# A hybrid encoder block on one core: the weights of five projections stored block by block

## The chip, the cores and the metric

The kernel runs on one core of a Trainium2 chip. The time is the device time of one execution in microseconds (us); smaller is better. The core has five engines, each with its own queue of instructions: TensorE (PE in the profile; PEld is its weight load), VectorE (DVE), ScalarE (ACT), GpSimd (POOL) and SyncE (SP), which only issues transfers. Transfers run on 16 DMA engines, whichever queue issued them. TensorE multiplies out of SBUF, the on-chip memory of 128 partitions, into PSUM.

## The reference

The input x is 2048 tokens of 1024 numbers, float32. One layer is computed:

```
h      = rms_norm(x, pre_mix_g)
proj   = h @ w_in                     # 1024 -> 5376: attention 1536, RWKV 1792, gates 2048
y_a    = chunk_band_attention(q, k, v, rel_bias)       # 8 heads, own chunk of 64 and 8 before it
y_b    = rwkv7_time_mix(p_rwkv, ...)                   # 8 heads, a delta-rule state over time
merged = sigmoid(gate_a) * (y_a @ proj_a) + sigmoid(gate_b) * (y_b @ proj_b)   # 512 -> 1024 each
x      = x + rms_norm(merged @ w_out, post_mix_g)      # 1024 -> 1024
u      = square(relu(rms_norm(x, pre_ffn_g) @ w_up)) @ w_down   # 1024 -> 4096 -> 1024
x      = x + rms_norm(u, post_ffn_g)
```

## The kernel before

**Precision.** Matrix products keep float32 accuracy by splitting each operand into a high and a low part. ScalarE casts the high part, VectorE subtracts to get the low one (`split`, L68), and `mm3` (L72) issues three products: high x high, high x low, low x high.

**Groups.** Tokens are worked on in four groups of 512 (`run`, L1480 on). For each group the RWKV branch comes first, then attention, then the merge with the branch projections and the output projection. The norm of the next group and the residual of the one before run in between. After the last group follows the feed-forward network, in two halves of two groups: `phase_up` (w_up) and a down phase (w_down) each. Both use sums and differences of quarter matrices to save products; the sums (`td`, t1 to t4 in the profile) and the activations (`ad`, `sd`) pass through DRAM.

**Where the weights come in.** Every weight block is 512 KB and is loaded by one transfer on SP's queue into a raw tile of 128 partitions x 1024 numbers (`wraw`); then it is split into `whi` and `wlo`, or in the up stage into `a1h`, `s12h` and so on. For w_in a block is 128 columns and all 1024 rows, eight rows to a partition (`block`, L82). For the branch projections it is 256 columns and 512 rows, for the output projection 256 rows and half of the columns (`blocks`, L85), for w_up 128 columns again (`load`, L1139). In DRAM the weights are the plain matrices, so a block's part of one partition lies in several pieces, one for each row.

**What sets the order.** The first group loads each block where it is used (`dense`, L109) and notes the order. From then on `ahead` (L99) runs one block in front: it loads and splits the next block before it hands over the present one. The pool has two raw tiles and two of each split tile, so a load waits for the split of the block two before it. In the feed-forward stages the raw tiles come from a pool of four, shared with the loads of w_down and of the activations.

The program is written in one order; a planner then fills each engine's queue when the program is built. It plays the program through with prices of its own for every instruction and transfer and takes what is ready first, so instructions of different steps can change places on an engine. Each engine runs its queue strictly in the order that came out. On ScalarE the casts of weights, the casts of `bl` (input of an up stage, L1090), the evictions of PSUM (`o` at L1002, `z` at L1190) and the activations stand in one line.

**Early in the program** the table of the attention bias is written out to DRAM by eight transfers (`build_bias`, L899) that share SP's queue with the first weight loads.

`layout` (L1536 on) arranges the inputs on the host before the launch: it drops the depth axis, reverses the bias table and flattens one vector. Its time is not part of the measurement.

Of the kernel before, what the change touches and what calls it, by code (L numbers as in the profile page):

```python
# [17 lines left out]
P = 128  # L18
D = 1024
KB = D // P  # L20
FF = 4096
HW = 512
NP = 4
# [29 lines left out]
class Block:  # L53
# [26 lines left out]
        return mm  # L80

    def block(self, col):  # L82
        return self.a["w_in"][:, col : col + P].rearrange("(k p) n -> p k n", p=P), KB, P

    def blocks(self):  # L85

        a = self.a
        for g in range(self.NG):
            if g:
                yield from map(self.block, self.order)  # L90
            for w in (a["proj_b"], a["proj_a"]):
                for i in range(KB // 2):
                    yield w[:, 2 * i * P : (2 * i + 2) * P].rearrange("(k p) n -> p k n", p=P), NP, 2 * P
            for n in range(2):
                for k in range(0, KB, 2):
                    rows = a["w_out"][k * P : (k + 2) * P, n * 512 : (n + 1) * 512]
                    yield rows.rearrange("(k p) n -> p k n", p=P), 2, 512

    def ahead(self):  # L99

# [1001 lines left out]
    def phase_up(self, half, zp, rp, cb, pn, early, sums=False):  # L1102
# [4 lines left out]
        tc, nc, a = self.tc, self.nc, self.a  # L1107
        KH = KB // 2
        lo4, hi4 = slice(0, KH), slice(KH, KB)
        with ExitStack() as ctx:  # L1110
# [27 lines left out]

            def load(fb):  # L1139
                raw = rp.tile([P, KB, P], F32, tag="raw", name="wraw")  # L1140
                nc.sync.dma_start(raw, a["w_up"][:, fb * P : (fb + 1) * P].rearrange("(k p) n -> p k n", p=P))
                return raw

            def parts(src, tag, n):
# [43 lines left out]
            for i in range(early):  # L1188
                A11, A12 = parts(load(2 * i), ("a1", "s12", "s3")[i % 3], KB)
                nc.scalar.copy(z[:, i], product(A11, B11, self.pd, "d"))  # L1190
                hidden(z[:, i], product(A12, B21, self.pd, "d"), 2 * i, 0)
                advance(ops, 1 + i % 2)
            advance(ops)

            for i in range(FF // P // 2):
                raw0, raw1 = load(2 * i), load(2 * i + 1)
                (a11, a12), (a21, a22) = ((x[:, lo4], x[:, hi4]) for x in (raw0, raw1))
                if i >= early:
# [24 lines left out]
                w = up.tile([P, G], F32, tag="w", name="w")  # L1223
# [312 lines left out]
def layout(inputs):  # L1536
    import numpy as np

    got = {}
    for name in _INS:  # L1540
        v = np.asarray(inputs["rel_bias" if name == "rel_rev" else name])[0]
        if name == "rel_rev":
            v = v[:, ::-1]
        if name == "r_k":
            v = v.reshape(-1)
        got[name] = np.ascontiguousarray(v)
    return got

# [16 lines left out]
```

## Time and profile before

| What | Value |
|---|---|
| time, median of 3 runs | 3363.93 us (3361.67 to 3368.97) |
| time of the profiled execution | 3364.64 us |
| its span, first to last instruction | 3362.8 us |
| TensorE busy | 3255.5 us (97%) |
| VectorE busy | 2282.5 us (68%) |
| ScalarE busy | 1461.8 us (43%) |
| DMA packets | 403538, 478.42 MB, mean 142 GB/s |
| mean granted TensorE clock | 0.990 |

The span is shorter than the execution's time by 1.84 us, which lie around it. "Busy" counts an engine's own instructions and leaves out waits and the issuing of transfers. A matmul's end is modelled, so a busy TensorE need not be at its peak rate. In a row of waits stand who waited, for whom, the total in us, the number of waits and the longest. In a row of a timeline stand start and length in us, engine, line, operation, tiles and shapes; a bracket holds how long the engine had been idle and what ended that. An "x3" at the end of such a row merges three instructions.

### The profile page before, as it was taken

How to read it: one execution, taken by the hardware profiler on the slowest of the kernel's cores; microseconds unless marked ns; L12 is line 12 of the kernel's file. 1: busy time of each engine (PE TensorE's matmuls, PEld its weight loads, DVE VectorE, ACT ScalarE, POOL GpSimd, SP SyncE). 2: the span in 40 equal slices, each digit the busy share in tenths (PEclk: the TensorE clock that was granted, in tenths of full speed). 3: DMA queues.
4: the chain of work that ended last, by engine and by line, in shares of the span. 5: the costliest groups of instructions: out<-in, count | busy, mean ns of one | idle time of the engine just before them, and what ended most of it. 6: DMA issues, size and time to landing. Idle time of an engine off the chain costs nothing. (4 is left out here: it accounts for less than half of the span.)

```text
span 3362.8 us, 49354 instructions
## 1 busy us (share of the span) xinstructions
PE 3255.5 (97%) x19089; PEld 2614.3 (78%) x19089; DVE 2282.5 (68%) x3806; ACT 1461.8 (43%) x2331; POOL 393.7 (12%) x732
## 2 busy tenths in 40 slices
PE   7999999999999999999999999999999999999998
PEld 5777777777777777777777777888888877888887
DVE  5774556675665774665774675877877777776778
ACT  4434534444644434644434644333431244453432
POOL 2110002110012210012210000111200010100002
PEclk9999999999999999999999999999999999999999
DMA  5224343235264225354224266434756374554443
GB/s 150 85 77 144 110 138 116 64 95 174 96 224 130 76 85 166 105 203 154 79 82 151 85 206 232 123 124 143 267 175 200 109 239 155 171 170 158 145 156 125
DMA packets 403538, 478.42 MB, mean 142 GB/s; under 512 B 17437, under 2 KB 304353, under 8 KB 400617
## 3 DMA queue, kind: packets, MB, share of 16 engines
q1 hardware_dynamic: 348712, 364.10, 34.4%
q0 software_dynamic: 18688, 63.98, 5.0%
q10 hardware_dynamic: 35904, 47.20, 4.0%
q8 instruction: 151, 2.47, 0.3%
q14 instruction: 83, 0.67, 0.1%
HBM read 355.64 MB, written 122.71 MB: 142 GB/s over the span
## 5 line engine op out<-in xcount | busy, mean ns | idle before, releaser
L78 PE MATMUL psd<-hh,whi 128*128 128x512 f32 x1344 | 545.2, 406 | 9.9 <-ACT whi L69 6.6
L78 PE MATMUL psd<-hl,whi 128*128 128x512 f32 x1344 | 541.9, 403 | 0.0
L78 PE MATMUL psd<-hh,wlo 128*128 128x512 f32 x1344 | 539.0, 401 | 0.8 <-DVE wlo L70 0.8
L69 ACT CAST whi<-wraw 128x1024 fp32r<-128x1024 f32 x232 | 243.5, 1050 | 529.9 <-PE psd L78 420.8
L78 PE MATMUL ps_dn<-fop 128*128 128x512 f32 x1920 | 439.8, 390 | 2.6 <-DVE u L1268 2.1
L70 DVE TENSOR_TENSOR wlo<-wraw,whi 128x1024 fp32r<-128x1024 f32 x232 | 283.0, 1220 | 212.0 <-ACT whi L69 191.0
L78 PEld LDWEIGHTS ps_dn<-fop 128*128 128x128 f32 x1920 | 359.4, 188 | 79.2 <-DVE u L1268 2.9
L78 PEld LDWEIGHTS psd<-hh,whi 128*128 128x128 f32 x1344 | 257.3, 191 | 66.2 <-ACT whi L69 7.4
L78 PEld LDWEIGHTS psd<-hh,wlo 128*128 128x128 f32 x1344 | 257.1, 191 | 56.8 <-issue 3.5
L78 PEld LDWEIGHTS psd<-hl,whi 128*128 128x128 f32 x1344 | 257.4, 192 | 51.4 <-issue 2.1
L78 PE MATMUL ps_dn<-fop,fop 128*128 128x512 f32 x1008 | 228.6, 389 | 0.0
L78 PEld LDWEIGHTS ps_dn<-fop,fop 128*128 128x128 f32 x1008 | 189.2, 188 | 39.3
L1268 DVE TENSOR_TENSOR u<-u,ps_dn 128x512 f32<-128x512 f32 x240 | 160.4, 683 | 53.9 <-PE ps_dn L78 53.2
L869 DVE CUSTOM_DVE_ANT_0 sc<-bias,ps_s 128x640 f32<-128x640 f32 (+4 forms) x128 | 94.0, 735 | 55.5 <-PE ps_s L863 47.0
L69 ACT CAST fop<-wdraw 128x1024 fp32r<-128x1024 f32 x40 | 41.9, 1047 | 190.8 <-PE ps_dn L78 104.5
L874 ACT ACTIVATE sc<-sc,mn 128x640 f32<-128x640 f32 (+4 forms) x128 | 97.8, 764 | 35.4 <-DVE mn L869 30.1
L996 PE MATMUL ps_o<-whi,mh 128*128 128x512 f32 x256 | 102.8, 402 | 4.7 <-ACT o L1002 4.2
L69 ACT CAST s12h<-s 128x1024 fp32r<-128x1024 f32 x32 | 33.7, 1054 | 169.1 <-PE ps_u L78 169.1
L996 PE MATMUL ps_o<-wlo,mh 128*128 128x512 f32 x256 | 102.4, 400 | 1.2 <-DVE wlo L70 1.2
L78 PE MATMUL ps_p<-yh,whi 128*128 128x512 f32 x256 | 102.0, 398 | 1.1 <-DVE th L962 1.1
L78 PE MATMUL ps_p<-yh,wlo 128*128 128x512 f32 x256 | 102.0, 399 | 0.0
L78 PE MATMUL ps_p<-yl,whi 128*128 128x512 f32 x256 | 101.5, 396 | 0.0
(378 smaller groups left out, 6755.3 us busy)
## 6 DMA issues: line engine op xcount, KB each, us to landing
wraw<-in_w_in_dram SPq DMA_DIRECT2D x168, 512.0 KB
wraw<-in_w_up_dram SPq DMA_DIRECT2D x80, 512.0 KB
ar<-sd SPq DMA_DIRECT2D x21, 1024.0 KB
wdraw<-in_w_down_dram SPq DMA_DIRECT2D x40, 512.0 KB
araw<-ad SPq DMA_DIRECT2D x40, 512.0 KB
gd<-gate ACTq DMA_DIRECT2D x64, 256.0 KB
wraw<-in_w_out_dram SPq DMA_DIRECT2D x32, 512.0 KB
ad<-r POOLq DMA_DIRECT2D x64, 256.0 KB, 2.7
```

What stands on the lines that cost most here:

```text
L69: self.nc.scalar.copy(hi, src)
L70: self.nc.vector.tensor_tensor(lo, src, hi.bitcast(F32), ALU.subtract)
L78: mm = nc.tensor.matmul(ps, l, r, start=start and n == 0, stop=stop and n == last).ins
L869: nc.vector.tensor_tensor_reduce(sc[:, 0:n], bias[:, s0:640], pss[:, c0 : c0 + n], 1.0, 3.0e38, ALU.add, ALU.min, mn,)
L874: nc.scalar.activation(sc[:, 0:n], sc[:, 0:n], AF.Exp, scale=-1.0, bias=mn, accum_out=sm)
L996: nc.tensor.matmul(ps[t], l[:, k, ts], r[:, k % 2], start=k == 0 and j == 0, stop=k == KB - 1 and j == 2)
L1268: nc.vector.tensor_tensor(u[t][:, ns], u[t][:, ns], ps, ALU.add)
```

## The change

The five weight arrays are stored in DRAM block by block in the order in which a tile holds them, so that a block's part of a partition is 1024 numbers, 4 KB, in a row. The values, the tiles, the number of transfers, their size and their places in the program's text stay the same; the access pattern of 312 loads becomes a plain one, and the host arranges the arrays.

```diff
     def block(self, col):
-        return self.a["w_in"][:, col : col + P].rearrange("(k p) n -> p k n", p=P), KB, P
+        return self.a["w_in"][col // P], KB, P
...
             for w in (a["proj_b"], a["proj_a"]):
                 for i in range(KB // 2):
-                    yield w[:, 2 * i * P : (2 * i + 2) * P].rearrange("(k p) n -> p k n", p=P), NP, 2 * P
+                    yield w[i], NP, 2 * P
             for n in range(2):
                 for k in range(0, KB, 2):
-                    rows = a["w_out"][k * P : (k + 2) * P, n * 512 : (n + 1) * 512]
-                    yield rows.rearrange("(k p) n -> p k n", p=P), 2, 512
+                    yield a["w_out"][n, k // 2], 2, 512
...
             def load(fb):
                 raw = rp.tile([P, KB, P], F32, tag="raw", name="wraw")
-                nc.sync.dma_start(raw, a["w_up"][:, fb * P : (fb + 1) * P].rearrange("(k p) n -> p k n", p=P))
+                nc.sync.dma_start(raw, a["w_up"][fb])
                 return raw
...
+        if name in ("w_in", "w_up"):
+            v = v.reshape(KB, P, -1, P).transpose(2, 1, 0, 3)
+        if name in ("proj_a", "proj_b"):
+            v = v.reshape(NP, P, -1, 2 * P).transpose(2, 1, 0, 3)
+        if name == "w_out":
+            v = v.reshape(KB // 2, 2, P, 2, 512).transpose(3, 0, 2, 1, 4)
         got[name] = np.ascontiguousarray(v)
     return got
```

## The prediction

> **What bounds the kernel now.** I read the page first, then TensorE's waits, then the stretches in which the DMA engines are full, and last the places where the two meet.
>
> ```profile
> span 3362.8 us, 49354 instructions
> PE 3255.5 (97%) x19089; PEld 2614.3 (78%) x19089; DVE 2282.5 (68%) x3806; ACT 1461.8 (43%) x2331; POOL 393.7 (12%) x732
> DMA packets 403538, 478.42 MB, mean 142 GB/s; under 512 B 17437, under 2 KB 304353, under 8 KB 400617
> ```
>
> TensorE is busy for 3255.5 of 3362.8 us, so all its idle time is 107.3 us. A change that only makes transfers shorter can win no more than the part of it that hangs on transfers, and what follows from that idling. Two rows of TensorE's waits, and one of ScalarE's:
>
> ```profile
> PE ps_t L570 <- DVE X L549: 26.8, 8, 3.9
> PE pstr L145 <- DVE x L307: 10.1, 1, 10.1
> ```
> ```profile
> ACT whi L69 <- PE psd L78: 420.8, 136, 8.8
> ```
>
> The two longest waits of TensorE have nothing to do with weights (the inverse on VectorE, the first norm). And ScalarE's cast of a weight block waits 136 times for TensorE to free the buffer, 420.8 us in all: in steady state the load has long landed. A load that lands sooner there only lies longer, so I count nothing for it; these 420.8 us are the work that hides it, and were that cover gone, the whole change per load would count.
>
> **The change part by part.** No instruction is added or removed: the same loads carry the same bytes into the same tiles on the same queue.
>
> ```profile
> wraw<-in_w_in_dram SPq DMA_DIRECT2D x168, 512.0 KB
> wraw<-in_w_up_dram SPq DMA_DIRECT2D x80, 512.0 KB
> wraw<-in_w_out_dram SPq DMA_DIRECT2D x32, 512.0 KB
> wraw<-in_proj_b_dram SPq DMA_DIRECT2D x16, 512.0 KB
> wraw<-in_proj_a_dram SPq DMA_DIRECT2D x16, 512.0 KB
> ```
>
> What changes is the pieces. A block of w_in or w_up is 128 partitions x 8 pieces of 512 B: 248 x 1024 = 253,952 pieces. The branches have 32 x 512 of 1 KB = 16,384, the output projection 32 x 256 of 2 KB = 8,192; together 278,528 of the page's 403,538 packets. Afterwards it is 312 x 128 = 39,936 pieces of 4 KB, and the page should show 164,946 packets. The reordering of the arrays is done on the host, ahead of the launch, and costs no device time.
>
> What such a load costs, before and after, I bound by stretches in which one kind dominates (columns: stretch, length, busy time of PE, PEld, DVE, ACT, POOL, granted clock, DMA share, GB/s):
>
> ```profile
> 100.00:200.00 100.00, 95.50 (x848) 76.06 (x846) 73.09 (x160) 44.49 (x80) 17.42 (x31) 0.97 0.21 65
> 2010.00:2020.00 10.00, 8.71 (x38) 6.65 (x37) 6.46 (x6) 5.04 (x5) 0.71 (x1) 1.00 1.03 302
> 2640.00:2660.00 20.00, 20.00 (x90) 16.53 (x89) 13.28 (x19) 3.89 (x4) 0.00 (x0) 1.00 0.29 83
> 2740.00:2750.00 10.00, 7.75 (x35) 6.11 (x34) 7.65 (x8) 8.25 (x11) 0.00 (x0) 1.00 1.03 414
> ```
>
> The first is an RWKV stage with w_in's 512-byte pieces and little else: 65 / 0.21 = 310 GB/s for full engines. The third holds the down projection's loads, which lie as 4 KB in a row already: 83 / 0.29 = 286 GB/s. So with half-empty engines long pieces are not quicker: 524,288 B are 1.69 us of full engines in the one and 1.83 us in the other, 0.14 us **worse**. In the second and fourth the engines are full. Mostly pieces of 512 B and 2 KB move 302 GB/s, mostly pieces of 4 KB (the inputs t1 to t4 of the up stage) 414 GB/s: 1.74 us a load against 1.27, a gain of **0.47 us**. Both hold other traffic, so this is an estimate from four rows. I take 0.47 us, because each place in which a load reaches TensorE lies in a full stretch; the loss of 0.14 us is the lower end.
>
> There are four such places.
>
> *A, the third block of the first group.*
>
> ```profile
> 33.24 64.08 SPq L63 DMA_DIRECT2D wraw<-in_w_in_dram  x11
> 43.62 1.04 ACT L69 CAST whi<-wraw 128x1024 fp32r<-128x1024 f32 x1
> 45.13 1.04 ACT L69 CAST whi<-wraw 128x1024 fp32r<-128x1024 f32 x1 [0.47 <-DMA wraw<-in_w_in_dram]
> 44.72 0.59 PE L78 MATMUL psd<-hh,whi 128*128 128x512 f32 x1 [4.95 <-ACT whi L69]
> ```
>
> The second cast waits for its landing, so the first block landed about one transfer earlier, near 43.6, some 10 us after its issue. It queues behind the copies of the bias table, which do not change; only its own transfer shrinks. I take 0.47 us; all of 4.95 is the upper end.
>
> *B and C, from the last merge into the first up stage.*
>
> ```profile
> 2001.51 7.48 SPq L1141 DMA_DIRECT2D wraw<-in_w_up_dram  x3
> 2014.17 0.37 SPq L63 DMA_DIRECT2D wraw<-in_w_out_dram  x1
> 2015.90 1.57 SPq L1141 DMA_DIRECT2D wraw<-in_w_up_dram  x2
> 2019.45 2.32 SPq L63 DMA_DIRECT2D wraw<-in_w_out_dram  x1
> 2021.82 1.94 SPq L1098 DMA_DIRECT2D bl<-ht  x3
> ```
> ```profile
> 2010.89 1.05 ACT L69 CAST a1h<-wraw 128x1024 fp32r<-128x1024 f32 x1 [4.72 <-DMA wraw<-in_w_up_dram]
> 2028.64 1.04 ACT L1090 CAST bh<-bl 128x1024 fp32r<-128x1024 f32 x1 [7.50 <-DMA bl<-ht]
> ```
> ```profile
> 2012.93 0.51 PE L996 MATMUL ps_o<-whi,mh 128*128 128x512 f32 x1 [0.54 <-ACT whi L69]
> 2014.19 0.50 PE L996 MATMUL ps_o<-wlo,mh 128*128 128x512 f32 x1 [0.75 <-DVE wlo L70]
> 2030.23 0.50 PE L996 MATMUL ps_o<-whi,mh 128*128 128x512 f32 x1 [3.73 <-ACT o L1002]
> 2031.66 0.79 PE L996 MATMUL ps_o<-whi,mh 128*128 128x512 f32 x1 [0.47 <-ACT o L1002]
> ```
>
> B: the cast of a1 stands ahead of the output projection's cast on ScalarE and waits for a w_up load; TensorE then idles 0.54 + 0.75 us. Two changed loads (a block of w_out, the first of w_up) are in the way: 2 x 0.47 = 0.94 of the 1.29 us. C: the cast of bl stands ahead of the PSUM evictions and waits 7.50 us; TensorE idles 3.73 + 0.47. The load of bl is old in form, but four changed loads issued from 2014.17 on lie before it in the queue: 4 x 0.47 = 1.88 of the 4.20 us (the upper end is all 4.20, if the gains of B's loads add up to here). The 7.48 us for three issues also show SP held by a full queue; with an eighth of the pieces that should vanish, but what is issued sooner then waits in the queue instead, so it counts nothing.
>
> C has a consequence. The clock after it, and after a shorter idle time elsewhere:
>
> ```profile
> 2030.00:2032.00 2.00, 1.30 (x4) 0.83 (x5) 1.79 (x2) 2.00 (x5) 0.00 (x0) 0.88 1.04 393
> 2032.00:2034.00 2.00, 2.00 (x6) 1.52 (x6) 0.82 (x2) 2.00 (x4) 0.00 (x0) 0.50 0.93 250
> 2034.00:2036.00 2.00, 2.00 (x8) 1.62 (x7) 2.00 (x3) 1.42 (x2) 0.00 (x0) 0.76 0.32 22
> 2750.00:2758.00 8.00, 8.00 (x37) 6.63 (x36) 7.08 (x9) 7.76 (x12) 0.00 (x0) 1.00 1.13 344
> ```
>
> After 3.73 us idle the granted clock falls, and 2 x (0.12 + 0.50 + 0.24) = 1.72 us are lost; after the 2.25 us of place D it stays at 1.00. Shortened by 1.88 us, C's idle time falls under 2.25: I count **1.72 us** more. A, still above 4 us, keeps its dip.
>
> *D, the start of the second up stage.*
>
> ```profile
> 2730.05 3.02 SPq L1141 DMA_DIRECT2D wraw<-in_w_up_dram  x2
> 2734.46 1.83 SPq L1130 DMA_DIRECT2D t2l<-td  x2
> 2741.75 1.05 ACT L1090 CAST t2h<-t2l 128x1024 fp32r<-128x1024 f32 x1 [2.42 <-DMA t2l<-td]
> 2749.12 0.50 PE L78 MATMUL ps_u<-bh,s3h 128*128 128x512 f32 x1 [2.25 <-ACT z L1190]
> ```
>
> Two w_up loads lie ahead of t2, whose cast delays ScalarE's eviction of z: 0.94 of the 2.25 us.
>
> The sum: 0.47 + 0.94 + 1.88 + 1.72 + 0.94 = **5.95 us**. The profiled execution took 3364.64 us (its span and 1.84 us around it), so 3358.7; it lies 0.71 above the median of the runs, which gives 3358.0. I predict 3358.5. The ends: all idle time of the four places and C's dip, 4.95 + 1.29 + 4.20 + 2.25 + 1.72 = 14.4 us, or 3350; and nine loads (1 + 2 + 4 + 2) at 0.14 us worse, 1.3 us, or 3366.
>
> [...]
>
> **The rivals.** *No change.* The loads may be no quicker even with full engines: 302 against 414 GB/s may come from the stores in the first stretch (the combined sums go out there), and the half-empty stretches say 310 against 286. Then the time is 3364.6, or 3366 by the lower end. [...]
>
> *More than the transfers.* The order in which each engine's queue is filled comes from a planner that prices every transfer. In A, ScalarE's casts wait in line with work of other steps. If shorter prices also move casts and evictions past each other, the four places vanish altogether: 3350. For it speaks that each of them is ScalarE's order as much as a late load; against it, that nothing shows that the planner prices pieces.
>
> *Slower, by the same planner.* If it believes the loads earlier than they come, it puts more casts ahead of PSUM evictions on ScalarE, as bl's cast in C does. Each such inversion costs what C costs now, 4.20 + 1.72 = 5.92 us; it decides from the point at which a cast's load lands after the eviction behind it is due. One would eat the gain (3364.6); three would give 3358.7 + 17.8 = 3376. Against it speaks that in the steady state loads land long before they are due.
>
> **How the numbers follow.** The forecast, a gain of 2 to 9 us: 0.48; no change: 0.19; more than the transfers: 0.18; slower by inversions: 0.15. About 0.2%, 6.7 us, is what a measurement of this kernel can tell from no change. The forecast lies just inside it, and about 0.22 of its 0.48 lies beyond 6.7 us; with the second rival that makes faster 0.40. Slower is 0.13 (two inversions or more), the same 0.47. The range reaches from 3350 to 3369, where one inversion beside lost gains would end.
>
> **What would show it.** The packets must fall to about 164,946; else the change does not do what it says. A's idle time should stay above 4 us, B's fall under 0.5, C's to about 2 us with a clock of 1.00 behind it, D's to about 1.3; full stretches with the new loads should move near 400 GB/s. TensorE's idle time should fall from 107.3 to about 103. The prediction is wrong if these places keep their waits, or if the engines' orders differ and new waits of TensorE on casts or evictions appear.

## The result, and the profile after

| | before | after |
|---|---|---|
| time, median | 3362.38 us (3359.79 to 3371.8, 9 runs) | 3355.02 us (3349.97 to 3357.79, 9 runs) |
| span of the profiled execution | 3362.8 us | 3353.1 us |
| TensorE busy / idle in the span | 3255.5 / 107.3 us | 3254.7 / 98.4 us |
| DMA packets | 403538 | 164945 |

The ratio is 0.9975, with a 95% interval from 0.9967 to 0.9984: faster by 0.25%, just over what can be told from no change. Two further comparisons of the same two kernels, described below, gave 0.9974 and 0.9971. The forecast was 3358.5 us, 3.5 us too slow and inside its range.

The head of the page of the changed kernel, the lines that answer to those shown of before:

```profile
span 3353.1 us, 49354 instructions
PE 3254.7 (97%) x19089; PEld 2612.5 (78%) x19089; DVE 2281.7 (68%) x3806; ACT 1461.6 (44%) x2331; POOL 391.8 (12%) x732
DMA packets 164945, 478.42 MB, mean 143 GB/s; under 512 B 17436, under 2 KB 34016, under 8 KB 162024
```

The same instructions move the same bytes in 164,945 packets (forecast: 164,946). TensorE's busy time is as it was, so the profiled gain is idle time: 107.3 - 98.4 = 8.9 of 9.7 us of span. On each of the five engines the instructions stand in the same order as before; only the shape of the 312 loads differs. From line 96 on, line numbers are one lower than before (L996 is L995, L1090 is L1089).

The timeline of the changed kernel at the places A to D (start, length, engine, line, operation, tiles; in the bracket how long the engine had been idle, and what ended it):

```profile
41.82 0.63 ACT L400 ACTIVATE E<-tw 128x512 f32<-128x512 f32 x1 [1.90 <-DVE tw L396]
42.36 0.60 ACT L535 CAST X<-x 128x512 f32<-128x512 bf16 x1
42.87 2.23 ACT L69 CAST whi<-wraw 128x1024 fp32r<-128x1024 f32 x2
43.96 0.79 PE L78 MATMUL psd<-hh,whi 128*128 128x512 f32 x1 [4.95 <-ACT whi L69]
...
2003.54 1.05 ACT L69 CAST a1h<-wraw 128x1024 fp32r<-128x1024 f32 x1 [3.19 <-DMA wraw<-in_w_up_dram]
2011.96 0.33 SPq L63 DMA_DIRECT2D wraw<-in_w_out_dram  x1
2012.34 1.69 SPq L1097 DMA_DIRECT2D bl<-ht  x3
2019.47 1.04 ACT L1089 CAST bh<-bl 128x1024 fp32r<-128x1024 f32 x1 [6.03 <-DMA bl<-ht]
2021.05 0.50 PE L995 MATMUL ps_o<-whi,mh 128*128 128x512 f32 x1 [1.90 <-ACT o L1001]
2022.48 0.51 PE L995 MATMUL ps_o<-whi,mh 128*128 128x512 f32 x1 [0.47 <-ACT o L1001]
...
2740.25 0.50 PE L78 MATMUL ps_u<-bh,s3h 128*128 128x512 f32 x1 [0.95 <-ACT z L1189]
```

A's 4.95 us stand as before. B's matmul waits of 0.54 and 0.75 us are gone from the list. C fell from 3.73 + 0.47 to 1.90 + 0.47, D from 2.25 to 0.95.

At C the difference stands on SP. Before, SP took 2.32 us to issue the block of w_out ahead of bl (the prediction's row at 2019.45), here 0.33 us, so bl is issued sooner. Counted from its own issue, bl's first block is not there sooner: its cast starts after 2028.64 - 2021.82 = 6.82 us before, after 2019.47 - 2012.34 = 7.13 us here.

The windows of the changed kernel (stretch, length, busy time of PE, PEld, DVE, ACT, POOL, granted clock, DMA share, GB/s), and under them the first of these stretches in the kernel before:

```profile
2008.00:2036.00 28.00, 25.62 (x105) 20.40 (x104) 13.55 (x12) 10.43 (x13) 0.40 (x1) 0.94 0.64 243
2010.00:2020.00 10.00, 9.15 (x41) 7.25 (x39) 3.16 (x3) 1.58 (x2) 0.00 (x0) 1.00 1.01 384
2740.00:2750.00 10.00, 9.75 (x43) 8.09 (x44) 9.38 (x11) 9.16 (x13) 0.00 (x0) 1.00 0.99 396
```
```profile
2008.00:2036.00 28.00, 22.51 (x89) 17.31 (x88) 13.13 (x13) 12.87 (x15) 0.71 (x1) 0.94 1.00 306
```

The full stretches move 384 and 396 GB/s. But the mean clock around C is 0.94 in both kernels: the dip behind C, which the forecast had struck out, is still there.

**A fifth place.** The list of four was one short. The timeline of the kernel before, near the end of the second up stage, then that of the changed kernel:

```profile
2838.08 1.57 SPq L1141 DMA_DIRECT2D wraw<-in_w_up_dram  x2
2847.89 1.05 ACT L69 CAST a1h<-wraw 128x1024 fp32r<-128x1024 f32 x1 [9.64 <-DMA wraw<-in_w_up_dram]
2849.94 0.50 PE L78 MATMUL ps_u<-t2h,s12h 128*128 128x512 f32 x1 [1.10 <-ACT s12h L69]
2852.58 0.50 PE L78 MATMUL ps_u<-t2h,s12l 128*128 128x512 f32 x1 [1.92 <-DVE s12l L70]
2855.44 0.50 PE L78 MATMUL ps_u<-t3h,s3h 128*128 128x512 f32 x1 [0.30 <-ACT s3h L69]
2856.72 0.50 PE L78 MATMUL ps_u<-t3h,s3l 128*128 128x512 f32 x1 [0.54 <-DVE s3l L70]
```
```profile
2829.14 1.53 SPq L1140 DMA_DIRECT2D wraw<-in_w_up_dram  x2
2837.92 1.05 ACT L69 CAST a1h<-wraw 128x1024 fp32r<-128x1024 f32 x1 [8.61 <-DMA wraw<-in_w_up_dram]
2842.61 0.79 PE L78 MATMUL ps_u<-t2h,s12l 128*128 128x512 f32 x1 [1.91 <-DVE s12l L70]
```

Call it E. ScalarE's cast of a1 starts 9.81 us after SP began to issue the two loads before, 8.78 us after; the casts of s12 and s3 stand behind it, and TensorE waits for them: 3.86 us in all before, 1.91 us after.

### The profile page after: what moved, and what is told of

Read it like the earlier page. It is cut to its first block, busy times and chain, and to the rows that moved or that the text cites. A ratio compares the mean times of both kernels' runs of the same rounds, so it can differ in the third digit from the quotient of the medians.

```text
span 3353.1 us, 49354 instructions
## 1 busy us (share of the span) xinstructions
PE 3254.7 (97%) x19089; PEld 2612.5 (78%) x19089; DVE 2281.7 (68%) x3806; ACT 1461.6 (44%) x2331; POOL 391.8 (12%) x732
## 2 busy tenths in 40 slices
DMA packets 164945, 478.42 MB, mean 143 GB/s; under 512 B 17436, under 2 KB 34016, under 8 KB 162024
## 5 line engine op out<-in xcount | busy, mean ns | idle before, releaser
L995 PE MATMUL ps_o<-whi,mh 128*128 128x512 f32 x256 | 102.6, 401 | 2.4 <-ACT o L1001 2.4
L995 PE MATMUL ps_o<-wlo,mh 128*128 128x512 f32 x256 | 102.3, 400 | 0.5 <-DVE wlo L70 0.4
L995 PE MATMUL ps_o<-whi,ml 128*128 128x512 f32 x256 | 101.7, 397 | 0.0
```

Source lines behind the costliest of these rows:

```text
L995: nc.tensor.matmul(ps[t], l[:, k, ts], r[:, k % 2], start=k == 0 and j == 0, stop=k == KB - 1 and j == 2)
```

## The experiments

The edits are shown against the kernel before where a part of the change is made alone, against the changed kernel where something is added. Each ratio is to the kernel before, with its 95% interval.

**One array at a time.** Only w_in in blocks:

```diff
-        return self.a["w_in"][:, col : col + P].rearrange("(k p) n -> p k n", p=P), KB, P
+        return self.a["w_in"][col // P], KB, P
```

> Only w_in is stored block by block (168 of the 312 loads); branches, output projection and w_up as before. Theory 'full stretches' (a shorter load counts only where the DMA engines are full and TensorE waits behind it): of the four places only A has a w_in load, so at most 0.5 us is gained, ratio 0.9998 to 1.000. Rival 'every load' (w_in's loads also bring something in the RWKV stages, which hold most of them): 3 to 5 us, ratio 0.9985 to 0.999. Rival 'clock chance' (the gain is a luckier set of clock dips in the RWKV stages, not the transfers): nothing, 1.000, but a spread of 3 us or more between executions.

Only w_up in blocks:

```diff
-                nc.sync.dma_start(raw, a["w_up"][:, fb * P : (fb + 1) * P].rearrange("(k p) n -> p k n", p=P))
+                nc.sync.dma_start(raw, a["w_up"][fb])
```

> Only w_up is stored block by block (80 loads). Theory 'full stretches': places B, C and D gain, about 0.5 + 1.0 to 2.0 + 1.0 to 1.3 us, without the loads of w_out: 2.5 to 4 us, ratio 0.9988 to 0.9993; TensorE's waits at D fall from 2.25 to about 1 us, C's from 3.73 to about 2.5. Rival 'every load': 1 to 2 us, by its share of the loads. Rival 'clock chance': 1.000.

Only the branches and the output projection:

```diff
-                    yield w[:, 2 * i * P : (2 * i + 2) * P].rearrange("(k p) n -> p k n", p=P), NP, 2 * P
+                    yield w[i], NP, 2 * P
...
-                    yield rows.rearrange("(k p) n -> p k n", p=P), 2, 512
+                    yield a["w_out"][n, k // 2], 2, 512
```

> Only the branches and the output projection are stored block by block (64 loads). Theory 'full stretches': B and C gain by the loads of w_out in front of them, at most 0.5 + 1.0 us, D nothing: 0.5 to 1.5 us, ratio 0.9995 to 0.9999. Rival 'every load': 1.5 us, 0.9995, so this run alone does not tell the two apart. Rival 'clock chance': 1.000.

And the whole change again:

> The changed kernel once more, unchanged: a second profile of it beside the first and a time next to the three parts. Theory 'full stretches': the waits of TensorE at A to D are the same as in the first profile within 0.2 us, the clock dips in the RWKV stages are others; ratio 0.9970 to 0.9985, near the sum of the three parts' gains. Rival 'clock chance': ratio 0.998 to 1.000, and the difference from the first profile is as large as that between the kernels.

| Blocks | time, median | ratio |
|---|---|---|
| w_in alone | 3361.49 us | 1.0002 (0.9992 to 1.0011) |
| w_up alone | 3358.46 us | 0.9988 (0.9980 to 0.9997) |
| branches, output projection alone | 3361.63 us | 0.9995 (0.9986 to 1.0005) |
| all | 3354.22 us | 0.9974 (0.9965 to 0.9983) |

w_in has 168 of the 312 loads and is worth nothing that can be measured; its interval just leaves out the 0.9985 to 0.999 of the rival 'every load'. w_up alone is the one part with an interval below 1. Timeline rows of w_up alone, at C and E:

```profile
2014.93 0.38 SPq L63 DMA_DIRECT2D wraw<-in_w_out_dram  x1
2023.83 0.50 PE L996 MATMUL ps_o<-whi,mh 128*128 128x512 f32 x1 [1.71 <-ACT o L1002]
2025.27 0.50 PE L996 MATMUL ps_o<-whi,mh 128*128 128x512 f32 x1 [0.47 <-ACT o L1002]
...
2846.58 0.50 PE L78 MATMUL ps_u<-t3h,s3l 128*128 128x512 f32 x1 [0.54 <-DVE s3l L70]
```

and of the branches and output projection alone:

```profile
2029.17 0.50 PE L995 MATMUL ps_o<-whi,mh 128*128 128x512 f32 x1 [3.03 <-ACT o L1001]
...
2849.52 0.50 PE L78 MATMUL ps_u<-t2h,s12l 128*128 128x512 f32 x1 [1.91 <-DVE s12l L70]
```

C's first wait is short (1.71) where w_up lies in blocks and long (3.03) where it does not. With w_up alone SP issues the block of w_out ahead of bl in 0.38 us, although w_out lies in its old order there; with the branches and the output projection alone that issue takes 2.44 us. So C is w_up's. At E it is 0.82 us in all with w_up's blocks (0.28 + 0.54) and 3.21 us without (1.30 + 1.91), but with w_in alone, w_up in its old order, it is as short as in the first profile of after:

```profile
2849.90 0.50 PE L78 MATMUL ps_u<-t2h,s12l 128*128 128x512 f32 x1 [1.91 <-DVE s12l L70]
```

So these runs alone do not settle E. The three parts add up to -0.02 + 0.12 + 0.05 = 0.15%, the whole is 0.26%; with some 0.09% of uncertainty on each, whether the parts together bring more than their sum stays open.

**How much differs between two executions of one kernel.** The kernel before, profiled a second time:

> The kernel before, unchanged, for a second profile of it: which of its differences from the changed kernel are differences between executions. Theory 'full stretches': TensorE's waits at A to D are those of the first profile within 0.2 us (4.95; 0.54 and 0.75; 3.73 and 0.47; 2.25), while the clock dips in the RWKV stages fall elsewhere and are worth up to 1.7 us each. Rival 'clock chance': some of the four waits themselves move by a microsecond or more.

Its rows at A, C and E:

```profile
44.78 0.80 PE L78 MATMUL psd<-hh,whi 128*128 128x512 f32 x1 [6.22 <-ACT whi L69]
...
2027.84 0.80 PE L996 MATMUL ps_o<-whi,mh 128*128 128x512 f32 x1 [4.01 <-ACT o L1002]
...
2848.17 0.51 PE L78 MATMUL ps_u<-t2h,s12l 128*128 128x512 f32 x1 [1.90 <-DVE s12l L70]
```

The changed kernel a third time, beside the later experiments:

> The changed kernel once more, beside the three others, for a third profile of places A to D. Expected: 0.9974 of the kernel before within 0.0009. A above 4 us, B under 0.5, C's first wait 1.9 within 0.3, D anywhere from 0.9 to 1.9 (the kernel before showed 2.25 and 1.15). If C's wait is 3 us or more here, the gain of place C was chance.

It took 3354.68 us, 0.9971 (0.9959 to 0.9982). Its rows at C, D and E:

```profile
2025.35 0.50 PE L995 MATMUL ps_o<-whi,mh 128*128 128x512 f32 x1 [1.55 <-ACT o L1001]
...
2744.89 0.50 PE L78 MATMUL ps_u<-bh,s3h 128*128 128x512 f32 x1 [2.53 <-ACT z L1189]
...
2847.33 0.50 PE L78 MATMUL ps_u<-t3h,s3h 128*128 128x512 f32 x1 [0.30 <-ACT s3h L69]
2848.61 0.50 PE L78 MATMUL ps_u<-t3h,s3l 128*128 128x512 f32 x1 [0.54 <-DVE s3l L70]
```

All five profiles of the two kernels, TensorE's idle time in us at each place (the sum of the brackets), from rows like these:

| Execution | A | B | C | D | E | all idle time |
|---|---|---|---|---|---|---|
| before | 5.19 | 1.29 | 4.20 | 2.25 | 3.86 | 107.3 |
| before, again | 6.22 | 1.00 | 4.01 | 1.15 | 1.90 | 104.8 |
| after | 4.95 | 0 | 2.37 | 0.95 | 1.91 | 98.4 |
| after, again | 5.73 | 0.47 | 2.39 | 1.87 | 1.10 | 99.5 |
| after, third | 4.95 | 0.43 | 2.02 | 2.53 | 0.84 | 101.0 |
| mean after - mean before | -0.5 | -0.85 | -1.85 | +0.1 | -1.6 | -6.4 |

Only B and C hold up fully: no execution of after reaches the lowest of before there. At E the mean falls, but the values meet (1.90 before, 1.91 after). Over all profiles of whole kernels here, E is 1.90 to 3.86 us in the five with w_up in its old order, 2.8 on the mean, and 0.82 to 2.66 us in the eight with its blocks, 1.4 on the mean; so a gain there is likely, its size uncertain. D's fall from 2.25 to 0.95 was two draws from one range: before shows 1.15 as well, after 2.53. That the waits would repeat within 0.2 us failed at A, D and E.

**What the pieces cost by themselves.** In this kernel no layer is computed. It only loads blocks of w_up through SP's queue, 24 in 512-byte pieces (a pitch of 16 KB in DRAM), 24 as 4 KB in a row, then both once more beside stores, and 8 of each one after the other:

```diff
+        stream(nc, fp, "a", "short_full", 8, short, acc)
+        stream(nc, fp, "a", "long_full", 8, long, acc)
+        stream(nc, fp, "a", "short_store", 8, short, acc, sd, z)
+        stream(nc, fp, "a", "long_store", 8, long, acc, sd, z)
+        stream(nc, fp, "b", "short_one", 1, short[:8], acc)
+        stream(nc, fp, "b", "long_one", 1, long[:8], acc)
```

> The disputed cost by itself. No layer is computed: the program loads w_up blocks of 512 KB, in 512-byte pieces (short) or as 4 KB in a row (long), 24 of each through eight buffers, so that the queues are full; then the same with one store of 512 KB beside every second load; then eight of each one by one through a single buffer. Theory 'full stretches': full queues 1.7 to 1.8 us a load for short and 1.25 to 1.4 for long, a difference of 0.4 to 0.5 us, with stores beside about the same difference; one by one the two land within 0.3 us of each other. Rival 'stores': full short and full long are equal within 0.1 us, and only with stores beside them does one differ. Rival 'every load': one by one, too, long is quicker by 0.4 us or more.

The bytes moved by slices of 6.6 us on its page, the issues in its timeline, and the DMA view's median from issue to landing:

```profile
GB/s 187 409 409 410 410 408 325 290 290 290 290 373 410 409 409 402 293 290 290 290 290 290 349 410 409 411 408 153 140 115 123 130 123 145 158 158 212 405 405 325
```
```profile
98.31 46.40 SPq L20 DMA_DIRECT2D short_store<-in_w_up_dram  x24
144.80 26.74 SPq L20 DMA_DIRECT2D long_store<-in_w_upb_dram  x24
```
```profile
short_one<-in_w_up_dram SPq DMA_DIRECT2D x8, 512.0 KB, 4.0
long_one<-in_w_upb_dram SPq DMA_DIRECT2D x8, 512.0 KB, 3.3
```

The stores, on a queue of their own, had all been issued within 36 us, so they ran beside the first stretch of short pieces and spoiled that one (its 409 GB/s hold both), while the stretches named for stores are clean. There 24 loads in short pieces, from 98.31 on, run at 290 GB/s, and in long ones, from 144.80 on, at 409 to 411. That is 524,288 B in 1.81 against 1.28 us: 0.53 us a load with full queues. Alone, a load lands 0.7 us sooner, more than the 0.3 us that theory 'full stretches' allowed. So long pieces are quicker in both cases, and the rival by which the 302 GB/s came from stores falls. Whether the length of the pieces or their pitch makes the 290 is not separated.

**A's wait: the queue or ScalarE's order.** The eight transfers that write out the bias table go to ScalarE's queue:

```diff
         for h in range(8):
-            nc.sync.dma_start(
+            nc.scalar.dma_start(
                 self.skew[h].rearrange("(q m) -> q m", m=769)[:, 0:768], band[h][None, :].to_broadcast((P, 768))
```

> The changed kernel with one more edit: the eight transfers that write out the bias table are issued on ScalarE's queue instead of SP's, so that the first weight loads no longer stand behind them. It is about place A (TensorE idle 4.95 and 5.73 us in the two profiles of the changed kernel). The prediction held that the block lands late there because it queues behind these eight transfers. By that theory the wait falls under 1 us, its clock dip goes, and the time is 4 to 7 us under the changed kernel's, about 0.9955 of the kernel before. The rival: the cast is late because it stands in ScalarE's order behind an activation that itself waits 1.9 us for VectorE's scan; then a wait of 4 us or more on ScalarE stays near 40 us and the time is the changed kernel's, about 0.9974. The planner may move the loras' products among the first group's; that is told from the waits.

3348.6 us, 0.9950 (0.9936 to 0.9964): 6.1 us under the changed kernel of the same comparison. Its timeline on ScalarE, and two windows:

```profile
34.36 1.05 ACT L69 CAST whi<-wraw 128x1024 fp32r<-128x1024 f32 x1
...
43.78 0.64 ACT L400 ACTIVATE E<-tw 128x512 f32<-128x512 f32 x1 [1.58 <-DVE tw L396]
```
```profile
40.00:44.00 4.00, 4.00 (x19) 3.27 (x18) 3.54 (x4) 2.31 (x4) 1.25 (x1) 1.00 0.82 257
44.00:48.00 4.00, 4.00 (x19) 3.29 (x18) 2.40 (x3) 3.12 (x5) 1.40 (x2) 1.00 0.28 107
```

TensorE does not stop between 40 and 48 us, and the clock stays at 1.00. Both theories had a part in it: the loads are issued 7 us sooner, and the planner, which prices the queues, put the third block's cast (34.36) ahead of the activation into tile E (43.78) behind which it had stood. With the order of the changed kernel left as it was, the earlier load alone was not tried.

The same edit on the kernel before, weights in their old order:

> The kernel before, weights in their old order, with the bias table's transfers on ScalarE's queue. It tells whether place A's wait has to do with the blocks' order at all. If the two are independent, A's wait goes here too, the time is 5 to 7 us under the kernel before (0.9980 to 0.9985), places B and C stay as in the kernel before (ps_o on o 3 us or more), and the blocks' order is worth 0.9970 to 0.9976 on top of it. If short pieces at A decide as well, its wait stays at 2 us or more here and the ratio is above 0.999.

3355.54 us, 0.9981 (0.9972 to 0.9990). At A and C:

```profile
44.32 1.04 ACT L69 CAST whi<-wraw 128x1024 fp32r<-128x1024 f32 x1 [5.08 <-DMA wraw<-in_w_in_dram]
45.41 0.51 PE L78 MATMUL psd<-hh,whi 128*128 128x512 f32 x1 [1.37 <-ACT whi L69]
...
2020.40 0.50 PE L996 MATMUL ps_o<-whi,mh 128*128 128x512 f32 x1 [3.07 <-ACT o L1002]
```

Here a cast does wait for the load of w_in and TensorE behind it, 1.37 us and, on wlo, 0.52; with the blocks a later cast waits 0.79 us and TensorE not at all. So the pieces of w_in count at A once ScalarE's order no longer covers them. Both kernels with this edit stand in the ratio 0.9950 / 0.9981 = 0.9969, the change's worth again.

**What is left of C.** The casts of bl go to GpSimd, so that they no longer stand ahead of the evictions on ScalarE:

```diff
-            self.split_here(bh[:, ks], bl[:, ks])
+            self.nc.gpsimd.tensor_copy(bh[:, ks], bl[:, ks].bitcast(F32))
+            self.nc.vector.tensor_tensor(bl[:, ks], bl[:, ks].bitcast(F32), bh[:, ks].bitcast(F32), ALU.subtract)
```

> The changed kernel with one more edit: the four casts of bl at the start of the up stages go to GpSimd instead of ScalarE. It is about what is left of place C, 1.90 + 0.47 us in the changed kernel's profiles. Theory: the cast, waiting for its load, stands ahead of the PSUM evictions on ScalarE, and nothing else holds them; then both waits of ps_o on o go (under 0.3 us), and the time is 2.4 us less, up to 4 with the clock's dip, 0.9963 to 0.9968 of the kernel before. Rival: the evictions wait for something else as well, or GpSimd's casts come so late that the products of the up stage wait for bh; then a wait of 2 us or more stands within 15 us behind the old one, and the time is the same as the changed kernel's, 0.9974, or above.

3360.44 us, 0.9992 (0.9983 to 1.0001): the gain is lost. Its rows:

```profile
2017.41 2.63 ACT L1001 COPY o<-ps_o 128x512 f32<-128x512 f32 x4 [2.35 <-PE ps_o L995]
...
2029.21 0.80 PE L995 MATMUL ps_o<-wlo,mh 128*128 128x512 f32 x1 [4.13 <-DVE wlo L70]
```

ScalarE evicts at once now, but the wait has moved: VectorE's subtraction for bl, waiting for GpSimd's cast, stands ahead of that for wlo, and TensorE idles 4.13 us there, 1.8 us more than at C in the changed kernel. That is a part of the 5.8 us lost. The planner changed VectorE's order at the second up stage too, where TensorE waits 3.15 us for u at 2446 us (1.52 in the changed kernel); the rest was not pinned down. Rival and theory were each half right: the waits on o went, and a new one came 12 us behind the evictions. Both edits together:

> The changed kernel with both edits, the bias table's transfers on ScalarE's queue and bl's casts on GpSimd. If the theories of A and C both hold, 6 to 10 us under the changed kernel, 0.9945 to 0.9955 of the kernel before; if neither, 0.9974. The sum of what the two bring alone, within 2 us, is expected either way, since the places lie 1970 us apart.

3354.4 us, 0.9972 (0.9960 to 0.9983); 0.0022 above the first edit alone, as the second edit cost by itself (0.9992 - 0.9971 = 0.0021). Last, with the bias table on ScalarE's queue, bl's loads on GpSimd's:

```diff
-            self.nc.sync.dma_start(bl[:, ks].bitcast(F32), self.ht[g][:, ks])
+            self.nc.gpsimd.dma_start(bl[:, ks].bitcast(F32), self.ht[g][:, ks])
```

> The kernel with the bias table's transfers on ScalarE's queue and, in addition, the loads of bl issued from GpSimd's queue instead of SP's. It is about place C. In the kernel with the first edit alone ScalarE's cast of bl waits 5.94 us for its load and TensorE 1.81 + 0.47 us behind it. If what is left of C is the late issue (bl's loads stand on SP behind loads of w_out that wait for a buffer), the cast's wait falls under 3 us, TensorE's two waits of ps_o on o go, and the time is 2 to 4 us under that kernel's 3348.6, 0.9938 to 0.9945 of the kernel before. If what is left is the full transfer engines, the same bytes move and a wait of 1.5 us or more stays on ps_o or moves to the w_out blocks (waits on whi or wlo): 0.995.

3354.18 us, 0.9974 (0.9963 to 0.9984). Its rows:

```profile
2002.70 0.71 POOL L1083 DMA_DIRECT2D td<-cmb  x1 [13.32 <-DVE cmb L1082]
2003.39 2.18 POOL L1097 DMA_DIRECT2D bl<-ht  x4
2013.47 1.05 ACT L1089 CAST bh<-bl 128x1024 fp32r<-128x1024 f32 x1 [5.01 <-DMA bl<-ht]
2017.61 0.80 PE L995 MATMUL ps_o<-whi,mh 128*128 128x512 f32 x1 [3.45 <-ACT o L1001]
...
2435.11 10.93 PE L78 MATMUL ps_dn<-fop 128*128 128x512 f32 x36 [6.06 <-DVE u L1267]
```

The first block of bl lands 10.1 us after its issue. With the loads on SP's queue it was 7.1 us (issue at 2007.22, cast at 2014.28 in the kernel with the first edit alone). Issued 3.8 us earlier, it landed 0.8 us earlier, so the late issue is at most a small part of what is left of C. Whether the full transfer engines are, stays open: on GpSimd's queue the loads also stand behind a store of 1 MB (the first row). The second cast now stands ahead of the eviction, and TensorE's wait grew to 3.45 us. The planner also changed VectorE's order at the second up stage, and TensorE waits 6.06 us at 2435 for VectorE; the 0.0024 against the first edit alone is the sum of the two, and the run does not part them.

## Why the prediction was right, and where not

- **The packets, and no instruction moved.** As forecast. With the same order on every engine, the two rivals that needed the planner to reorder the kernel ("more than the transfers", "slower, by the same planner") fall: their condition was not met. The planner does react to a transfer put on another queue, as the later experiments show.
- **0.47 us a load with full engines.** Right in kind, a little small: 0.53 us measured by itself. The lower end, 0.14 us worse in half-empty stretches, was wrong: it compared two kinds of loads in two stages, and w_up's own blocks land 4.0 and 3.3 us after their issue, one at a time. The measured rate is 290 against 410 GB/s, 29% less; since the length of the pieces and their pitch were not parted, the run does not say what the length alone does.
- **Nothing in the steady state.** Right as far as can be told: w_in alone, 168 loads, 1.0002 (0.9992 to 1.0011).
- **A, 0.47 us.** The step failed by misreading a row. The first cast there had no bracket, so ScalarE had not waited for the load; I took the landing to be what set it. The wait of 4.95 us is the same to the hundredth in before, in after and in each of the three one-array kernels: it is ScalarE's order (the cast stands behind the activation into tile E, which waits 1.90 us for VectorE's scan). Only when the cast waits for its load too does it grow (5.73, 6.22). That moving the copies of the bias table would take it away, with 6.1 us, was not forecast.
- **B, 0.94 us.** Right: -0.85 us by the table. The cast of a1 starts 8.9 to 9.4 us after SP begins to issue the w_up loads where these lie in the old order, 7.9 to 8.5 us after it where they lie in blocks.
- **C, 1.88 us.** The amount is right, -1.85 us; the path is not. I added up shorter transfers ahead of bl in the queue and put SP's hold by a full queue at nothing, because what is issued sooner would wait in the queue instead. The runs show the reverse: SP takes 1.9 to 3.0 us to issue the block ahead of bl in five profiles with w_up in its old order and 0.33 to 0.38 us with its blocks, while bl's cast starts 6.1 to 6.8 us after bl's issue in the old order and 6.8 to 7.2 us with the blocks. The gain is the earlier issue. That it is w_up's blocks, two of the four loads, and not the output projection's, I had not parted.
- **C's clock dip, 1.72 us.** Failed. With 1.90 + 0.47 us idle the clock still falls (0.94 in the stretch of 28 us, as before), against my reading that 2.25 us are short enough. In the third execution of after 1.55 + 0.47 us were enough (0.94), while the kernel with w_up alone idled 1.71 + 0.47 us there and kept 1.00, so the length alone does not decide. Nor does it at D: in the kernel with w_up alone 2.05 us of idling were followed by matmuls of 0.61 to 0.63 us from 2740.89 us on, for 3.4 us, then by one of 0.52 and by others of 0.39 and 0.40; in the third execution of after 2.53 us of idling, which end at 2744.89, were followed by one of 0.50 and then by matmuls of 0.39 and 0.40. By the trace's record of the clock, in before and in the first execution of after every dip begins a whole multiple of 3.4133 us after the first one (up to 969 and 967 of them, off by at most 0.03 us). Whether it counts how an idle time lies in that grid, the runs do not settle: at A of the changed kernel one stretch of it was idle throughout (39.99 to 43.40 us) and a dip of 6.83 us begins at its end; at C none was, and the clock fell all the same (0.50 from 2023.13 to 2026.55 us).
- **D, 0.94 us.** Failed: no gain on the mean, and the wait scatters from 0.95 to 2.53 us in after. I took the two w_up loads ahead of t2 for what holds its landing. But t2's cast starts 7.29 and 6.18 us after t2's issue in before and 5.99, 6.92 and 7.29 us after it in after, whatever the form of those two. What sets it stays open.
- **"There are four such places."** E was missing, with 1.6 us on the mean. I had looked for stretches with full engines and did not go through the casts that wait longest for a load of w_up (9.64 us).
- **The sum.** 5.95 us forecast, 7.4 us between the medians (7.2 and 8.7 in the other two comparisons). B, C and E make 4.3 us of it. The rest, some 3 us, was not pinned down. On the mean of the profiles the span falls by 7.9 us: 6.4 us of idle time and 1.5 us of TensorE's busy time, and that busy time differs by 3.0 us among the three executions of after alone. Clock dips, which at a clock of 0.50 cost 1.7 us for each 3.41 us, come and go between executions of one kernel (from 2835 to 2845 us the clock is 0.87 in the first execution of after and 1.00 in the second), so a dip that differs in two profiles proves nothing of the change. That the total came near was in part luck: E and the unexplained rest stood in for what C's dip and D did not bring.

## What to carry to other kernels

A shorter load was worth here only what a cast waited for it, or for a transfer issued behind it (the 168 of w_in alone: 1.0002): list the casts whose bracket names a transfer, longest first, and price those alone; a cast without a bracket is held by its own engine's order, and there the order has to change (6.1 us here, as much as the whole forecast, by an edit that also brought the loads 7 us forward). Look at how long the issuing queue is held as well: at C that was the whole gain (2.32 us before, 0.33 us after). Handing a late cast to another engine moved the wait here to the engine that takes the next step (4.13 us of TensorE behind VectorE). And profile each kernel twice before a single wait's change is believed: waits here differ by 1 us or more from one execution to the next.

## What the runs showed of the hardware

- With a full queue, loads of 512 KB in 512-byte pieces at a pitch of 16 KB move 290 GB/s, in 4 KB pieces 409 to 411 GB/s.
- SP took 2.32 us to issue one load behind blocks in 512-byte pieces in before, 0.38 us to issue the same load behind blocks in 4 KB pieces in the kernel with w_up alone.
- In before and in the first execution of after the granted clock falls to 0.50 for 3.41 or 6.83 us at a time (12.5 and 11.2 us at the program's end), and the dips begin on a grid of 3.413 us. The length at one place differs between executions: at A it is 3.41 us in the first profile of before, where TensorE idles 5.19 us, and 6.83 us in after, where it idles 4.95 us; in the second profile of before the matmuls there are slow for at least 4.4 us (0.58 to 0.80 us each from 44.78 us on, 0.39 to 0.40 before and behind).
